# A hybrid decoder trunk on one Trainium2 core: the recurrent gate weights are fetched from ScalarE's queue, and the wide block products put their 512-column matmuls ahead of their 256-column ones

## The chip, the cores and the metric

The kernel runs on one core of one Trainium2 chip. The time is device microseconds (us) of one execution, and lower is better. Five engines work side by side, each in the order of its own list of instructions: TensorE (PE in the profile; its weight loads are the row PEld), VectorE (DVE), ScalarE (ACT), GpSimd (POOL) and SyncE (SP). They meet at semaphores: an instruction stands until the counts that it names are reached, and all that is behind it in its engine's list stands with it. Transfers (DMAs) are issued by an engine and carried by 16 shared DMA engines. SP and ACT issue into hardware queues (q1 and q10 in the profile), POOL into a software queue (q0); transfers that add into their target are all issued by POOL here.

## The reference, cut to what matters

One layer on 512 tokens of 1024 channels: a half-weighted SwiGLU feed-forward, a mixer of two branches, a second half-weighted SwiGLU, and a final norm, all in float32.

```python
for l in range(DEPTH):                                   # DEPTH = 1
    x = x + 0.5 * swiglu(rmsnorm(x, ffn1_norm[l]), ffn1_wg[l], ffn1_wu[l], ffn1_wd[l])
    x = x + hybrid_mixer(rmsnorm(x, mix_norm[l]), w_in[l], ...)
    x = x + 0.5 * swiglu(rmsnorm(x, ffn2_norm[l]), ffn2_wg[l], ffn2_wu[l], ffn2_wd[l])
return rmsnorm(x, final_norm)

def swiglu(x, w_gate, w_up, w_down):
    return (jax.nn.silu(x @ w_gate) * (x @ w_up)) @ w_down   # 1024 -> 2816 -> 1024

# in hybrid_mixer, the recurrent branch:
xr = causal_dwconv(xr, conv_w, conv_b)
r = jax.nn.sigmoid(block_diag_linear(xr, w_a, b_a))      # 16 blocks of 64 x 64
i = jax.nn.sigmoid(block_diag_linear(xr, w_x, b_x))
a = jnp.exp(-8.0 * r * softplus(-lam))
h = scan(h = a * h + jnp.sqrt(1 - a * a) * i * xr)
```

The mixer's other branch is an attention over the 128 keys of each query that an indexer picks; both branches are gated, added and projected.

## The kernel before, in words

**Precision.** Each float32 factor is split into a rounded high part and a rest. ACT makes the high part (names that end in h: `wh`, `xh`, `yh`, and `gw` for the gate weights' first half), DVE the rest (`wl`, `xl`, `yl`). Three matmuls then stand for one product: high by high, high by rest, rest by high. A matmul here has 128 rows of weights and 128, 256 or 512 moving columns.

**Stages.** The first feed-forward runs until about 355 us of the profiled execution, the mixer from there to about 700, the second feed-forward to the end. The last two carry most of this case.

**The mixer** is a list of 59 projection jobs (`ORDER`, L50; `run_jobs`, L1370). A job is 24 matmuls of 512 columns on one 512 KB block of weights, which SP fetches (`wr`), ACT rounds (`wh`) and DVE completes (`wl`); three raw buffers and three pairs of split buffers turn. Beside the jobs run small programs that hand work to the engines whenever a model of the engines' times (`Plan`, L85; `due`, L1180; `tick`, L1343) takes their inputs to be ready: the indexer's scores (`masks`, L1207, which multiplies the tiles `KI` and `QI`, takes the relu on ACT into `rl` and sums it on DVE into `am`), the attention heads (`head`, L1271: `pm`, `pth`), the recurrent branch (`recurrent`, L1528: `xc`, `xh`, `xl`) and the gate weights (`gate_weights`, L1150). The order is fixed when the program is built; the model only decides where in each list an instruction stands.

**The gate weights.** Eight times (t = 0 to 7), three jobs ahead of the job `x{t}`, `gate_weights` takes two slots, fetches 128 KB of weights into `gr`, lets ACT round them into the first half of `gw` and DVE put the rest into the second half. `recurrent` uses them in six matmuls of 512 columns (`mm<-xh,gw`). In the profile the fetch is POOL's line L158, `gr<-wrg`.

**POOL's queue.** During the mixer POOL also issues the transfers that build sums of the second feed-forward's weight blocks in HBM (`Blocks.stages`, L323: `scr<-w2u`, `scr<-scr`), each group waiting for the one before it.

**Hardware transfers and semaphores.** All transfers that SP and ACT issue share eight completion semaphores (DMAHW0 to DMAHW7), given out in the order in which the program was recorded. Before a transfer is issued, the earlier one on its semaphore must have landed, so a transfer stands until the one eight places ahead of it is in.

**The second feed-forward's first half** (`ffn_up`, L413, called with `blocks`) forms 18 pairs of weight blocks with seven products each, 126 products in all (`products`, L533). In such a wide product PE does, for j = 0 to 3, a matmul of 512 columns with `wh` (both halves of the moving tile `cm`) and one of 256 columns with `wl` (its first half), all into one PSUM bank. The first feed-forward calls the same function without `blocks` and uses 256 columns throughout.

Of the kernel before, what the change touches and what calls it, by code (L numbers as in the profile page):

```python
# [14 lines left out]
P = 128  # L15
S = 512
D = 1024
KD = D // P
# [157 lines left out]
def hybrid_kernel(ctx, tc, xt, vec, w1u, w1d, wm, wki, wrg, watt, wrnn, wout, w2u, w2d, gf, out):  # L176
    nc = tc.nc
    plan = Plan()
    V, A = plan.engine("DVE", nc.vector), plan.engine("ACT", nc.scalar)
    G, T = plan.engine("POOL", nc.gpsimd), plan.engine("PE", nc.tensor)  # L180
# [16 lines left out]
    moving = {}  # L197

    def nm(s):
        cnt[0] += 1  # L200
        return f"{s}_{cnt[0]}"

    def slot(dt=F32, name="s"):
        return plan.take("slot", big.tile([P, S], dt, tag="slot", name=nm(name)))
# [7 lines left out]
    def psum(tag="mm"):  # L212
        return psp.tile([P, S], F32, tag=tag, name=nm(tag))
# [71 lines left out]
    def waits(which, *tiles, aux=0, att=0, slots=0, key=None, mm=0, tmps=0, late=LATE):  # L285
        return which, tiles, aux, att, slots, key, mm, tmps, late
# [126 lines left out]
    def ffn_up(y, wu, n0, hs, g, waiting=(), given=(), ahead=None, blocks=None):  # L413
# [119 lines left out]
        def products(i):  # L533
            p, w = stream[i]
            o = ws[w]
            if p == 1:
                o.beta = psum("mm")
            elif p == 2:
                o.p2 = psum("aux")
            elif p == 5:  # L540
                o.gamma = psum("aux")
            both = {2: lambda: o.p2, 5: lambda: o.gamma, 3: lambda: o.gamma}.get(p, lambda: o.beta)()
            acc_ = both[:, lo]
            h, l = (t[:, i % 2 * H:(i % 2 + 1) * H] for t in units[i // 2])
            starts, opens = p in (1, 2, 5), dict(skip_group_check=p not in (1, 2, 5))
            for j in range(KD // 2):
                c = slice(j * P, (j + 1) * P)
                m = moving[{1: "n11", 2: "b21", 6: "t2", 5: "t1", 7: "r", 4: "q", 3: "n22"}[p]][j]
                if blocks:
                    T.matmul(both, h[:, c], m, start=starts and j == 0, stop=False, **opens)  # L550
                else:
                    T.matmul(acc_, h[:, c], m[:, lo], start=starts and j == 0, stop=False, **opens)
                    T.matmul(acc_, h[:, c], m[:, hi], start=False, stop=False, **opens)
                T.matmul(acc_, l[:, c], m[:, lo], start=False, stop=j == KD // 2 - 1, **opens)
# [98 lines left out]
        with tc.manual_schedule(engines=ENGINES):  # L653
# [34 lines left out]
            for i in range(len(stream)):  # L688
                products(i)
                if not i:  # L690
                    together(results_direct(len(direct) - 1))
                if blocks:
                    wide_step(i)
                elif i:
                    results(i - 1)
                if i + LEAD < len(stream):
                    if not blocks:
                        prepare(i + LEAD)
                elif not ahead or i + LEAD - len(stream) < PLAIN - f0:
                    halve(hs, f0 + i + LEAD - len(stream))  # L700
                if ahead:
                    ahead(i - len(stream))
                if i % 14 == 12 and i // 14 < f0:
                    halve(hs, i // 14)
                if blocks:
                    continue
                if i % 7 == 1 and len(ws) < count:
                    load_ = load(len(ws))
                next(load_, None)
# [214 lines left out]
    for k in range(KD):  # L924
        if k:
            Q.dma_start(x[k], xt[k])
        if k % CH == 0:
            c = slice(k * P, (k + CH) * P)
# [17 lines left out]
    for k in range(KD):  # L946
        y.append(norm_tile(k, V_G1, False))
        if k % CH == 0:
            c = slice(k * P, (k + CH) * P)
# [164 lines left out]
    with tc.manual_schedule(engines=ENGINES):  # L1114
# [3 lines left out]
        for i in range(last):  # L1118
            if i == 0:
                for k in ("pth", "ptl"):  # L1120
                    t = ptp.tile([P, NQ * S], F32, tag=k, name=nm("sm"))
# [28 lines left out]
    def gate_weights(t):  # L1150
        yield waits("PE", slots=2)
        r, w = slot(F32, "gr")[:, :2 * P], slot(F32R, "gw")
        h, l = w[:, :2 * P], w[:, 2 * P:]
        G.dma_start(r, wrg[t])
        yield waits("ACT", r)
        A.activation(h, r, AF.Copy)
        yield waits("DVE", h)
        V.tensor_sub(l, r, f(h))
        plan.drop(r)
        rgw[t] = h, l  # L1160
# [253 lines left out]
    for k in ("pth", "ptl"):  # L1414
        q = ptp.tile([P, NQ * S], F32R, tag=k, name=nm("QI"))
# [308 lines left out]
    for t in range(KD):  # L1724
        starts_.setdefault(max(0, order[f"x{t}"] - AHEAD), []).append(lambda t=t: gate_weights(t))
# [57 lines left out]
    def rows(m, half):  # L1783
        return xr[m // 2][:, m % 2, half * S:(half + 1) * S]
# [77 lines left out]
    with tc.manual_schedule(engines=ENGINES):  # L1862
# [19 lines left out]
        for m in range(2):  # L1882
            r = rows(m, 1)
# [66 lines left out]
```

## Time and profile before

| | us |
|---|---|
| three runs | 1075.64, 1078.17, 1075.22 |
| their median | 1075.64 |
| the profiled execution | 1079.05 |
| its span, from first to last instruction | 1077.2 |
| granted TensorE clock over the span | 0.995 |

The profiled execution is 3.4 us above the median of the runs, and 1.85 us of it lie outside its span. Busy time in the profile is a share of the span; an idle stretch is put down to whoever ended it. A row of the timeline has the start in us, the length in us, the engine, the line of the kernel, the operation, output<-inputs, and in brackets the idle time before it with its releaser. Where a helper records the operation, the line is that of the helper (L170 for computing, L158 for transfers), so tiles are told apart by name.

### The profile page before, as it was taken

What the parts mean: (1) busy time and instruction counts of PE and PEld (TensorE: products, weight loads), DVE (VectorE), ACT (ScalarE), POOL (GpSimd) and SP (SyncE); (2) the same over time, 40 slices, a digit from 0 to 9 for tenths busy, and PEclk for the clock granted to TensorE, in tenths of its full rate; (3) what the DMA queues carried; (4) which work ended last, traced back from release to release, by engine and by line L of the source; (5) the groups of instructions that cost most, each with busy time, mean ns of one, the idle gap of its engine ahead of it and who ended that gap; (6) DMA issues with size and microseconds to landing.
All of it is one profiled execution on the core that took longest, in us unless ns stands there. A gap on an engine that the chain in (4) does not pass through costs nothing.

```text
span 1077.2 us, 16865 instructions
## 1 busy us (share of the span) xinstructions
PE 1060.8 (98%) x5908; PEld 921.6 (86%) x5908; DVE 861.0 (80%) x1583; ACT 670.5 (62%) x1234; POOL 214.9 (20%) x283
## 2 busy tenths in 40 slices
PE   9999999999999999998999999999999999999997
PEld 7889999999999778886888888888888888888886
DVE  6687777779978878897889967765888888878865
ACT  6565555556566657865977574345666666666663
POOL 0161111102331113344443453000400000000020
PEclk9999999999999999999999999999999999999999
DMA  7297777738993597999999999433856565544673
GB/s 275 54 257 185 175 192 172 183 107 233 246 232 105 166 261 189 260 297 297 276 283 297 297 256 211 127 113 89 171 185 195 177 193 181 181 150 157 195 200 132
DMA packets 101012, 214.19 MB, mean 199 GB/s; under 512 B 12416, under 2 KB 20736, under 8 KB 100096
## 3 DMA queue, kind: packets, MB, share of 16 engines
q1 hardware_dynamic: 67632, 148.83, 42.2%
q0 software_dynamic: 32576, 63.46, 30.8%
q8 instruction: 46, 0.75, 0.3%
q10 hardware_dynamic: 720, 0.84, 0.2%
q14 instruction: 38, 0.31, 0.1%
HBM read 202.06 MB, written 56.62 MB: 240 GB/s over the span
## 4 chain that ended last, share of the span: by engine, by line
PE 78%; DMA 7%; DVE 6%; ACT 4%; issue 2%; POOL 1%; SPq 1%; ACTq 0%; POOLq 0%; DVEq 0%
PE mm L170 53%; PE aux L170 26%; DMA scr<-w2u 3%; DVE wl L170 2%; DMA gr<-wrg 1%; DMA sm<-w1d 1%; ACT wh L170 1%; DMA s<-w1d 1%; DMA QI<-qil 1%; SPq L158 1%; DVE ca L170 1%; DMA wr<-wm 0%; POOL scr L324 0%; DVE am L170 0%; DMA x<-xt 0%
## 5 line engine op out<-in xcount | busy, mean ns | idle before, releaser
L170 DVE TENSOR_TENSOR wl<-wr,wh 128x1024 fp32r<-128x1024 f32 (+2 forms) x253 | 258.0, 1023 | 88.5 <-ACT wh L170 86.4
L170 ACT ACTIVATE wh<-wr 128x1024 fp32r<-128x1024 f32 (+3 forms) x255 | 225.6, 890 | 82.0 <-PE aux L170 26.7
L170 PE MATMUL mm<-cm,wh 128*128 128x256 f32 (+1 forms) x1184 | 267.0, 311 | 0.6 <-ACT wh L170 0.3
L170 PE MATMUL mm<-cm,wl 128*128 128x256 f32 x736 | 207.8, 282 | 0.2 <-DVE wl L170 0.2
L170 PEld LDWEIGHTS mm<-cm,wh 128*128 128x128 f32 x1184 | 194.3, 191 | 15.4 <-ACT wh L170 0.5
L170 PE MATMUL mm<-yh,wh 128*128 128x512 f32 (+1 forms) x416 | 165.6, 398 | 2.0 <-ACT wh L170 1.4
L170 PE MATMUL mm<-yl,wh 128*128 128x512 f32 (+1 forms) x416 | 163.6, 394 | 0.5 <-DVE yl L170 0.5
L170 PE MATMUL mm<-yh,wl 128*128 128x512 f32 x408 | 160.6, 394 | 0.0
L170 PE MATMUL aux<-cm,wh 128*128 128x256 f32 (+1 forms) x664 | 160.2, 321 | 0.0
L170 PEld LDWEIGHTS mm<-cm,wl 128*128 128x128 f32 x736 | 140.4, 191 | 0.5 <-DVE wl L170 0.4
L170 PE MATMUL aux<-cm,wl 128*128 128x256 f32 x440 | 124.0, 282 | 0.0
L170 PEld LDWEIGHTS aux<-cm,wh 128*128 128x128 f32 x664 | 110.5, 191 | 10.1
L170 PEld LDWEIGHTS mm<-yh,wh 128*128 128x128 f32 (+1 forms) x416 | 78.8, 189 | 19.4 <-ACT wh L170 2.3
L170 PEld LDWEIGHTS mm<-yl,wh 128*128 128x128 f32 (+1 forms) x416 | 78.3, 188 | 16.3 <-DVE yl L170 1.2
L170 PEld LDWEIGHTS mm<-yh,wl 128*128 128x128 f32 x408 | 77.4, 190 | 16.8
L324 POOL DMA_DIRECT2D scr<-w2u x72 | 61.5, 965 | 113.6 <-DMA scr<-w2u 102.2
L170 PEld LDWEIGHTS aux<-cm,wl 128*128 128x128 f32 x440 | 83.8, 190 | 0.0
L158 POOL DMA_DIRECT2D cm<-h x16 | 13.8, 863 | 270.2 <-ACT cm L170 257.3
L170 PE MATMUL mm<-wh,cm 128*128 128x512 f32 x192 | 59.1, 389 | 0.0
L170 DVE TENSOR_TENSOR wl<-s,wh 128x512 fp32r<-128x512 f32 x72 | 49.3, 687 | 11.8 <-ACT wh L170 11.0
L170 ACT ACTIVATE wh<-s 128x512 fp32r<-128x512 f32 x72 | 43.7, 622 | 18.2 <-DVE s L170 14.5
L158 POOL DMA_DIRECT2D s<-w1u x32 | 30.1, 1105 | 108.8 <-DMA s<-w1u 51.3
(251 smaller groups left out, 2034.1 us busy)
## 6 DMA issues: line engine op xcount, KB each, us to landing
wr<-scr SPq DMA_DIRECT2D x104, 256.0 KB, 3.0
wr<-wm SPq DMA_DIRECT2D x39, 512.0 KB, 7.6
scr<-w2u POOLq DMA_DIRECT2D x72, 256.0 KB, 12.8
wr<-w2u SPq DMA_DIRECT2D x54, 256.0 KB, 3.0
scr<-scr POOLq DMA_DIRECT2D x52, 256.0 KB, 11.8
wr<-w1u SPq DMA_DIRECT2D x21, 512.0 KB, 5.1
wr<-w1d SPq DMA_DIRECT2D x18, 512.0 KB, 4.1
scr<-w2u SPq DMA_DIRECT2D x36, 256.0 KB, 9.1
```

The lines of the kernel that those rows point to most:

```text
L158: return self.engine.dma_start(out, src, **kw)
L170: return call(*args, **kw)
L324: plain, adds = nc.gpsimd.dma_start, lambda o, i: nc.gpsimd.dma_start(o, i, accum_op=ALU.add)
```

## The change

```diff
@@ -543,12 +543,12 @@
             acc_ = both[:, lo]
             h, l = (t[:, i % 2 * H:(i % 2 + 1) * H] for t in units[i // 2])
             starts, opens = p in (1, 2, 5), dict(skip_group_check=p not in (1, 2, 5))
-            for j in range(KD // 2):
+            ms = moving[{1: "n11", 2: "b21", 6: "t2", 5: "t1", 7: "r", 4: "q", 3: "n22"}[p]]
+            for j, m in enumerate(ms if blocks else ()):
+                T.matmul(both, h[:, j * P:(j + 1) * P], m, start=starts and j == 0, stop=False, **opens)
+            for j, m in enumerate(ms):
                 c = slice(j * P, (j + 1) * P)
-                m = moving[{1: "n11", 2: "b21", 6: "t2", 5: "t1", 7: "r", 4: "q", 3: "n22"}[p]][j]
-                if blocks:
-                    T.matmul(both, h[:, c], m, start=starts and j == 0, stop=False, **opens)
-                else:
+                if not blocks:
                     T.matmul(acc_, h[:, c], m[:, lo], start=starts and j == 0, stop=False, **opens)
                     T.matmul(acc_, h[:, c], m[:, hi], start=False, stop=False, **opens)
                 T.matmul(acc_, l[:, c], m[:, lo], start=False, stop=j == KD // 2 - 1, **opens)
@@ -1151,7 +1151,8 @@
         yield waits("PE", slots=2)
         r, w = slot(F32, "gr")[:, :2 * P], slot(F32R, "gw")
         h, l = w[:, :2 * P], w[:, 2 * P:]
-        G.dma_start(r, wrg[t])
+        nc.scalar.dma_start(r, wrg[t])
+        plan.copy(r, wrg[t], "POOL")
         yield waits("ACT", r)
         A.activation(h, r, AF.Copy)
         yield waits("DVE", h)
```

**The gate weights.** The eight transfers leave POOL's list and enter ACT's. The model of the engines' times still books them on POOL, so every other instruction keeps its place. On ACT's list, the place of the fifth transfer (t = 4, in the middle of the mixer) is this piece of the difference; `gw` is the rounding of the weights that `gr` brings, `wh` that of the next job's weights:

```order
 L170 ACTIVATE sg_5251<-mm_5174 128x512
 L170 ACTIVATE rl_5253<-aux_5212 128x512
+L1154 DMA gr_5265<-wrg 128x256
 L170 ACTIVATE gw_5266<-gr_5265 128x256
 L170 ACTIVATE wh_5276<-wr_5051 128x1024
```

The rounding that needs the transfer is now the instruction right behind its issue. The same on ACT at the seventh transfer (t = 6), which stands behind the gate `sg` of a finished job:

```order
 L170 ACTIVATE gu_5797<-gu_5797 128x512
 L170 ACTIVATE sg_5853<-mm_5809 128x512
+L1154 DMA gr_5862<-wrg 128x256
 L170 ACTIVATE gw_5863<-gr_5862 128x256
 L170 ACTIVATE wh_5872<-wr_5712 128x1024
```

Of the eight, t = 3 to 7 stand like this; at t = 0, 1 and 2 other work of ACT lies between. In the profile the moved transfer will carry its own line, L1154, as it no longer goes through the helper.

**The shared semaphores.** With eight more hardware transfers, the turn of DMAHW0 to DMAHW7 shifts for SP. Around the place where SP copies the indexer's queries into `QI`, one piece of SP's list before, with the semaphores that each transfer waits for:

```order
L158 DMA wr_4732<-wm 128x1024 [waits DMAHW5_49,DVE_49]
L158 DMA QI_4551<-qih_4645 32x512 [waits DMAHW6_49]
L158 DMA QI_4552<-qil_4683 32x512 [waits DMAHW7_49]
L158 DMA QI_4551<-qil_4646 32x512 [waits DMAHW0_49]
L158 DMA QI_4552<-qih_4682 32x512 [waits DMAHW1_49]
L158 DMA QI_4551<-qih_4645 32x512 [waits DMAHW2_49]
```

And the same transfers of SP in the changed kernel:

```order
L158 DMA wr_4732<-wm 128x1024 [waits DMAHW6_49,DVE_49]
L158 DMA QI_4551<-qih_4645 32x512 [waits DMAHW7_49]
L158 DMA QI_4552<-qil_4683 32x512 [waits DMAHW0_49]
L158 DMA QI_4551<-qil_4646 32x512 [waits DMAHW1_49]
L158 DMA QI_4552<-qih_4682 32x512 [waits DMAHW3_49]
L158 DMA QI_4551<-qih_4645 32x512 [waits DMAHW4_49]
```

SP skips DMAHW2, which one of ACT's transfers holds there: seven of SP's own transfers can be under way at such a place, where it was eight.

**The wide products.** On PE's list, the first product of the second feed-forward's stream (`cm` moving, `wh` and `wl` as weights):

```order
 L170 MATMUL mm_8647<-cm_8330,wh_8552 128x512
+L170 MATMUL mm_8647<-cm_8331,wh_8552 128x512
+L170 MATMUL mm_8647<-cm_8503,wh_8552 128x512
+L170 MATMUL mm_8647<-cm_8584,wh_8552 128x512
 L170 MATMUL mm_8647<-cm_8330,wl_8553 128x256
-L170 MATMUL mm_8647<-cm_8331,wh_8552 128x512
 L170 MATMUL mm_8647<-cm_8331,wl_8553 128x256
-L170 MATMUL mm_8647<-cm_8503,wh_8552 128x512
 L170 MATMUL mm_8647<-cm_8503,wl_8553 128x256
-L170 MATMUL mm_8647<-cm_8584,wh_8552 128x512
 L170 MATMUL mm_8647<-cm_8584,wl_8553 128x256
```

The eight matmuls are the same; the four of 512 columns come first. All 126 wide products change in this way, and nothing else on PE. DVE's list is unchanged.

## The prediction

> **What bounds the kernel now.** I read the page's busy table first, then PE's waits, then the tile `gr`, then ACT and PE in order of time around each gate-weight transfer.
>
> ```profile
> PE 1060.8 (98%) x5908; PEld 921.6 (86%) x5908; DVE 861.0 (80%) x1583; ACT 670.5 (62%) x1234; POOL 214.9 (20%) x283
> ```
>
> TensorE is busy for 98% of the span, so only two things can move the end: PE's idle time, and the pace of its matmuls. PE's longest wait, in the view of waits for PE alone (total, times, longest), and the rows of the view of the tile `gr`:
>
> ```profile
> PE aux L170 <- ACT pm L170: 4.0, 2, 3.4
> ```
>
> ```profile
> DMA gr<-wrg: 10.5, 3
> ...
> DMA to landing us min/median/max: 2.4/7.2/13.6
> ```
>
> Three of the eight roundings kept ACT waiting for their transfer, 10.5 us together (t = 5, 6, 7). The last of them is PE's longest wait. First ACT, then PE, then the stretches around it with the granted clock in the third column from the end:
>
> ```profile
> 501.44 0.60 ACT L170 ACTIVATE sg<-mm 128x512 f32<-128x512 f32 x1 [2.16 <-PE mm L170]
> 506.99 0.42 ACT L170 ACTIVATE gw<-gr 128x256 fp32r<-128x256 f32 x1 [4.95 <-DMA gr<-wrg]
> ```
>
> ```profile
> 508.70 0.33 PE L170 MATMUL aux<-ident,pm 128*128 128x128 f32 x1 [3.39 <-ACT pm L170]
> ```
>
> ```profile
> 505.00:509.00 4.00, 0.61 (x4) 0.30 (x3) 0.43 (x1) 2.01 (x6) 1.33 (x2) 1.00 1.08 306
> 509.00:513.00 4.00, 4.00 (x13) 3.16 (x12) 3.83 (x11) 3.95 (x7) 2.19 (x4) 0.60 1.10 245
> ```
>
> ACT was free at 502.04 and stood until the transfer was in; `pm`, behind `gw` on ACT, was what PE needed. PE lost 3.39 us, and then some (1 - 0.60) x 4.00 = 1.6 us more, as the granted clock fell to 0.60. So the most that the moved transfers can give back here is about 5 us.
>
> **The wide products.** PE in order of time, the first and last rows of 98 pairs of a 512-column and a 256-column matmul; of 25 steps from 512 to 512 columns in the mixer; of 18 steps from 256 to 256 at the end of the first feed-forward:
>
> ```profile
> 799.63 0.40 PE L170 MATMUL mm<-cm,wh 128*128 128x512 f32 x1
> ...
> 834.25 0.40 PE L170 MATMUL mm<-cm,wh 128*128 128x512 f32 x1
> ```
>
> ```profile
> 367.99 0.39 PE L170 MATMUL mm<-yl,wh 128*128 128x512 f32 x1
> ...
> 373.65 0.39 PE L170 MATMUL mm<-yh,wl 128*128 128x512 f32 x1
> ```
>
> ```profile
> 349.50 0.28 PE L170 MATMUL mm<-cm,wl 128*128 128x256 f32 x1
> ...
> 351.66 0.28 PE L170 MATMUL mm<-cm,wl 128*128 128x256 f32 x1
> ```
>
> A pair takes 34.62 / 98 = 0.3533 us; a step between equal widths takes 5.66 / 25 = 0.2264 and 2.16 / 18 = 0.1200, together 0.3464. Alternating costs 7 ns a pair. A product is 4 x 0.3533 = 1.413 us now; with the widths grouped it has three steps of each kind and one pair's worth of changes, 3 x 0.2264 + 3 x 0.1200 + 0.3533 = 1.393. Over 126 products that is 126 x 0.0207 = **2.6 us less**. The bounds are 0 (the 7 ns belong to these operands, not to the alternation) and 3.5 us (126 x 4 x 0.0069). I take 2.6.
>
> **How long a transfer takes on ACT's queue (L).** The trace has none of this kind in the mixer. From the view of transfers, with size and median us from issue to landing:
>
> ```profile
> gr<-wrg POOLq DMA_DIRECT2D x8, 128.0 KB, 7.2
> ...
> out<-o ACTq DMA_DIRECT2D x2, 256.0 KB, 2.4
> wr<-w1u ACTq DMA_DIRECT2D x2, 128.0 KB, 4.7
> ```
>
> ```profile
> 470.00:490.00 20.00, 19.43 (x91) 15.75 (x90) 18.60 (x47) 11.08 (x27) 9.22 (x13) 1.00 1.08 304
> ```
>
> The low end is 2.4, with the DMA engines nearly idle at the end of the program; the high end is 7.2, in POOL's queue. At t = 5 and 6 the engines are full (a share of 1.08). I take L = 4.7: same queue, same size, issued beside SP's loads. The Trainium skill, "DMA: Bandwidth & Descriptors", section "Anatomy of one DMA", fits 2.0 us plus the bytes over 436 GB/s, an estimate of 2.3 us here; the 2.4 of the first `gr` agrees, the median of 7.2 does not, and by that fit the time would be the first rival's.
>
> **What L does at each place.** At t = 3 to 7 the rounding stands right behind the issue, so ACT now stands for all of L, where POOL had issued early.
>
> At t = 2, ACT's wait behind one weight rounding is covered by the 2.55 us that it idles for PE anyway; t = 0 and 1 have some 9 us of other work:
>
> ```profile
> 392.85 1.20 ACT L170 ACTIVATE QS<-mm 64x512 fp32r<-64x512 f32 x2 [2.55 <-PE mm L170]
> ```
>
> At t = 3 nothing waited. ACT and PE:
>
> ```profile
> 399.99 0.43 ACT L170 ACTIVATE gw<-gr 128x256 fp32r<-128x256 f32 x1
> ...
> 401.63 1.06 ACT L170 ACTIVATE wh<-wr 128x1024 fp32r<-128x1024 f32 x1 [0.94 <-DMA wr<-wm]
> ...
> 403.12 0.64 ACT L170 ACTIVATE rl<-aux 128x256 f32<-128x256 f32 x2
> ```
>
> ```profile
> 406.13 0.51 PE L170 MATMUL aux<-KI,QI 128*128 128x384 f32 x2
> ```
>
> Of 4.7 us, 0.94 are idle time, and PE takes the bank that `rl` frees 2.37 us after `rl` (406.13 - 403.76). The rest is 1.4 us if all else stays, 0 if the weights' landing sets `wh` anyway; I take 0.7.
>
> At t = 4 nothing waited either, but DVE stood behind the `wh` that follows `gw` on ACT, and has almost no slack afterwards. DVE, then PE:
>
> ```profile
> 427.09 1.23 DVE L170 TENSOR_TENSOR wl<-wr,wh 128x1024 fp32r<-128x1024 f32 x1 [2.05 <-ACT wh L170]
> ...
> 432.87 1.23 DVE L170 TENSOR_TENSOR wl<-wr,wh 128x1024 fp32r<-128x1024 f32 x1 [0.30 <-ACT wh L170]
> ...
> 443.18 0.68 DVE L170 TENSOR_TENSOR xl<-xc,xh 128x512 fp32r<-128x512 f32 x1
> ```
>
> ```profile
> 445.38 0.39 PE L170 MATMUL mm<-xl,gw 128*128 128x512 f32 x1
> ```
>
> PE needs `xl` 1.52 us after it is made. 4.7 - 0.30 - 1.52 = **2.9 us**.
>
> At t = 5 and 6, ACT:
>
> ```profile
> 469.83 1.20 ACT L170 ACTIVATE QS<-mm 64x512 fp32r<-64x512 f32 x2 [0.33 <-PE mm L170]
> 474.31 0.42 ACT L170 ACTIVATE gw<-gr 128x256 fp32r<-128x256 f32 x1 [3.28 <-DMA gr<-wrg]
> ...
> 481.69 0.60 ACT L170 ACTIVATE sg<-mm 128x512 f32<-128x512 f32 x1 [1.37 <-PE mm L170]
> 484.59 0.42 ACT L170 ACTIVATE gw<-gr 128x256 fp32r<-128x256 f32 x1 [2.30 <-DMA gr<-wrg]
> ```
>
> ```profile
> 486.30 0.91 PE L170 MATMUL aux<-ident,pm 128*128 128x128 f32 x3 [0.56 <-ACT pm L170]
> ```
>
> At t = 5, `gw` starts at 471.03 + 4.7 = 475.7 instead of 474.31; the 1.4 us vanish in the 1.37 that ACT idles for PE before `sg`: 0. At t = 6 it starts at 482.29 + 4.7 = 487.0 instead of 484.59. PE already waits for `pm` behind it, so **2.4 us** arrive whole. At t = 7 it starts at 502.04 + 4.7 = 506.74 instead of 506.99: **0.25 us gained**, the stall and the dip of the clock stay.
>
> **SP's semaphores.** SP copies the indexer's queries back to back, 0.63 us apart, and PE uses them soon:
>
> ```profile
> 390.20 0.59 SPq L158 DMA_DIRECT2D QI<-qih  x1
> 390.90 0.52 SPq L158 DMA_DIRECT2D wr<-wm  x1
> 391.46 0.51 SPq L158 DMA_DIRECT2D QI<-qil  x1
> ```
>
> ```profile
> DMA to landing us min/median/max: 2.7/5.0/6.4
> ```
>
> ```profile
> 392.65 0.64 PE L170 MATMUL aux<-KI,QI 128*128 128x256 f32 x4
> ```
>
> Eight in flight cover 8 x 0.63 = 5.0 us, just the copies' median to landing; seven cover 4.4. If landing takes as long as before, two rounds lose 0.6 each, and up to 6.4 - 4.4 = 2.0 at the slowest; if it shortens with fewer in flight, nothing. Bounds 0 and 2.0; I take 0.9.
>
> **The sum.** 0.9 + 0.7 + 2.9 + 0 + 2.4 - 0.25 = 6.65 us more in the mixer, 2.6 less in the second feed-forward: **+4.05 us**. The profiled execution's 1079.05 becomes 1083.1; the median of the runs, 1075.64, becomes **1079.7**. POOL's list loses eight issues, which gives nothing: no row has PE waiting for POOL's sums.
>
> **The rivals.**
>
> *Faster: the transfer lands fast in a queue of its own.* It leaves the tail of POOL's queue, and at t = 7 the gain is L against 4.95. With L = 2.4: t = 4 costs 0.6, t = 6 0.1, t = 7 gives 2.55, and the stall, then 0.8 us, no longer brings the clock down: 1.6 more. Sum -3.45, with the products -6.05: 1069.6. It decides at about L = 3.2, where the total is -3. For it speaks that ACT's queue is empty; against it that all queues share engines that are full.
>
> *No change: L near 3.8.* 0.7 + 0.3 + 2.0 + 1.5 - 1.15 = 3.3, less 2.6: 1076.3. The two parts cancel.
>
> *The grouping changes nothing,* because the 7 ns belong to the operands: 1082.3. Against it: equal widths run at the same pace in three stages with other operands.
>
> *The dip of the clock goes,* since the stall at t = 7 is 3.14 us instead of 3.39: 1.6 less, 1078.1. The measured dip is the row of 0.60 above. The Trainium skill, "TensorE: Matmul & The Clock Gate", section "What's actually happening", halves the clock after an idle window of some 3.4 us; the trace agrees so far (3.39 us, 0.60), and by that rule a slightly shorter stall may escape, while the window's phase is free.
>
> **How the numbers follow.** Chances: the forecast 0.42 (L from 4.4 to 6); fast landing 0.14; cancelling 0.30; grouping without effect 0.08; the dip gone 0.06. About 0.3%, 3.2 us, is what a measurement of this kernel can tell from no change. Slower 0.42 + 0.08 = 0.50; same 0.30 + 0.06 = 0.36; faster 0.14. The ends of L alone would give 1069.6 and, at 7.2, over 1090; eight times in ten I expect L between 3.1 and 5.8, which is 1072.5 to 1085.0.
>
> **What would show it.** In the changed kernel: `gr` on ACT's queue with a median landing of 4 to 5.5 us; ACT waiting for `gr` five to six times, over 20 us in all; a PE wait of about 3 us at t = 6 and of about 3 at t = 7; PE held behind `xl` or `rl` near 430 to 450; 512-column steps of 0.2264 in the wide products, and a stretch of 126 products 2.6 us shorter. A median landing under 3.2, or PE's wait at t = 7 gone, would make the forecast wrong; so would wide products that still take 1.413.

## The result and the profile after

The changed kernel takes 1091.94 us in the median of four runs (1087.66 to 1095.08), the kernel before 1075.53. The ratio is 1.0144 with a 95% interval of 1.0106 to 1.0183: 1.4% slower, and above the forecast range of 1072.5 to 1085.0. The profiled executions differ by 12.7 us (1091.73 against 1079.05). The profiled execution of before lies 3.5 us above the median of its runs (all runs of before lie between 1071.95 and 1081.69), so the other 3.7 us of the medians' difference is not in these two traces.

The view of the tile `gr` in the changed kernel, and PE's waits (total, times, longest):

```profile
  DMA gr<-wrg: 24.4, 5
...
DMA to landing us min/median/max: 2.2/5.2/8.0
```

```profile
PE aux L170 <- ACT pm L170: 10.1, 2, 5.1
PE mm L170 <- ACT wh L170: 2.3, 3, 1.5
PE aux L170 <- ACT rl L170: 2.0, 1, 2.0
```

ACT waited 24.4 us instead of 10.5 us for the gate weights, five times instead of three, and PE 10.1 us instead of 4.0 us for the `pm` behind them; a wait of 2.0 us for `rl` is new. ACT in order of time, at t = 3, 4, 5, 6 and 7: the issue of each transfer (ACTq) and the rounding that needs it, with ACT's idle time in brackets; at t = 3 also the `rl` right behind the rounding:

```profile
400.87 0.33 ACTq L1154 DMA_DIRECT2D gr<-wrg  x1
...
406.65 0.42 ACT L170 ACTIVATE gw<-gr 128x256 fp32r<-128x256 f32 x1 [4.70 <-DMA gr<-wrg]
406.97 0.36 ACT L170 ACTIVATE rl<-aux 128x256 f32<-128x256 f32 x1
...
429.38 0.34 ACTq L1154 DMA_DIRECT2D gr<-wrg  x1
...
432.06 0.42 ACT L170 ACTIVATE gw<-gr 128x256 fp32r<-128x256 f32 x1 [1.08 <-DMA gr<-wrg]
...
475.02 0.34 ACTq L1154 DMA_DIRECT2D gr<-wrg  x1
...
483.03 0.42 ACT L170 ACTIVATE gw<-gr 128x256 fp32r<-128x256 f32 x1 [6.82 <-DMA gr<-wrg]
...
487.92 0.34 ACTq L1154 DMA_DIRECT2D gr<-wrg  x1
...
494.21 0.42 ACT L170 ACTIVATE gw<-gr 128x256 fp32r<-128x256 f32 x1 [5.19 <-DMA gr<-wrg]
...
512.60 0.33 ACTq L1154 DMA_DIRECT2D gr<-wrg  x1
...
519.83 0.42 ACT L170 ACTIVATE gw<-gr 128x256 fp32r<-128x256 f32 x1 [6.64 <-DMA gr<-wrg]
```

From issue to rounding it took 5.8, 2.7, 8.0, 6.3 and 7.2 us. PE in order of time shows what of this arrives. First t = 3, the last row ahead of the stall and the first behind it:

```profile
404.98 0.40 PE L170 MATMUL mm<-yh,wl 128*128 128x512 f32 x1
407.39 0.48 PE L170 MATMUL aux<-KI,QI 128*128 128x384 f32 x1 [2.02 <-ACT rl L170]
```

The wait ends with the `rl` that starts at 406.97, right behind the rounding. In the kernel before, the same two matmuls follow one another:

```profile
403.63 0.40 PE L170 MATMUL mm<-yh,wl 128*128 128x512 f32 x1
403.87 0.33 PE L170 MATMUL aux<-KI,QI 128*128 128x384 f32 x1
```

The distance between the two traces grows from 1.35 us to 3.52 us there. At t = 6 and t = 7, where the kernel before has its rows at 486.30 and 508.70:

```profile
495.92 1.06 PE L170 MATMUL aux<-ident,pm 128*128 128x128 f32 x3 [5.00 <-ACT pm L170]
...
521.54 0.48 PE L170 MATMUL aux<-ident,pm 128*128 128x128 f32 x1 [5.07 <-ACT pm L170]
```

The distance is 9.62 us and 12.84 us. Between these places it grows a second time, because the clock falls after each stall. The stretches behind the three stalls, the granted clock in the third column from the end:

```profile
407.30:411.00 3.70, 3.61 (x9) 2.95 (x10) 3.20 (x6) 2.58 (x6) 0.00 (x0) 0.55 0.14 18
...
494.00:498.00 4.00, 2.08 (x6) 1.63 (x7) 3.27 (x10) 3.05 (x8) 1.62 (x2) 0.50 1.08 288
...
521.00:525.00 4.00, 3.46 (x9) 2.79 (x10) 2.99 (x10) 3.95 (x10) 2.07 (x4) 0.50 1.09 236
```

Followed matmul by matmul, the distance is 1.4 us ahead of t = 3 (0.6 of it is there before the indexer's queries are used); the stall there adds 2.2 and the clock 1.7; t = 4 and 5 add nothing; t = 6 adds 4.4 and the clock 1.5; t = 7 adds 1.7, and the clock 0.9 beyond its dip in the kernel before. That makes 13.8 us; the second feed-forward gives back 1.2, and 12.6 us are left at PE's last matmul.

### The profile page after: what moved, and what is told of

It is laid out like the page before. It is cut to its first block, busy times and chain, and to the rows that moved or that the text cites. A ratio compares the mean times of both kernels' runs of the same rounds, so it can differ in the third digit from the quotient of the medians.

```text
span 1090.0 us, 16858 instructions
## 1 busy us (share of the span) xinstructions
PE 1064.0 (98%) x5908; PEld 925.2 (85%) x5908; DVE 861.4 (79%) x1583; ACT 669.7 (61%) x1234; POOL 209.8 (19%) x275
## 4 chain that ended last, share of the span: by engine, by line
PE 85%; DVE 6%; DMA 6%; ACT 2%; issue 2%; SPq 0%; POOL 0%; ACTq 0%; POOLq 0%; DVEq 0%
PE mm L170 59%; PE aux L170 26%; DMA gr<-wrg 2%; DVE wl L170 2%; DMA sm<-w1d 1%; ACT wh L170 1%; DMA s<-w1d 1%; DMA cm<-cb 1%; DVE yl L170 0%; DMA x<-xt 0%; DVE yf L170 0%; DVE ca L170 0%; DVE h L170 0%; ACT cm L170 0%; ACT yh L170 0%
## 5 line engine op out<-in xcount | busy, mean ns | idle before, releaser
L170 PE MATMUL mm<-cm,wh 128*128 128x256 f32 (+1 forms) x1184 | 242.0, 310 | 0.5 <-ACT wh L170 0.5
L170 PEld LDWEIGHTS mm<-cm,wh 128*128 128x128 f32 x1184 | 189.4, 191 | 8.3 <-ACT wh L170 0.7
L170 PE MATMUL mm<-cm,wl 128*128 128x256 f32 x736 | 172.7, 282 | 0.2 <-DVE wl L170 0.2
L170 PE MATMUL aux<-cm,wh 128*128 128x256 f32 (+1 forms) x664 | 141.4, 319 | 0.3 <-DMA cm<-cb 0.3
L170 PEld LDWEIGHTS mm<-cm,wl 128*128 128x128 f32 x736 | 130.2, 191 | 6.6 <-DVE wl L170 0.4
L170 PEld LDWEIGHTS aux<-cm,wh 128*128 128x128 f32 x664 | 106.9, 191 | 5.4 <-DMA cm<-cb 0.5
L170 PE MATMUL aux<-cm,wl 128*128 128x256 f32 x440 | 97.7, 282 | 0.0
L324 POOL DMA_DIRECT2D scr<-w2u x72 | 65.8, 1062 | 116.5 <-DMA scr<-w2u 113.3
L170 PEld LDWEIGHTS aux<-cm,wl 128*128 128x128 f32 x440 | 76.1, 190 | 4.6
L158 POOL DMA_DIRECT2D cm<-h x16 | 13.7, 857 | 269.1 <-ACT cm L170 256.1
L170 DVE TENSOR_TENSOR wl<-s,wh 128x512 fp32r<-128x512 f32 x72 | 49.3, 688 | 11.8 <-ACT wh L170 11.0
## 6 DMA issues: line engine op xcount, KB each, us to landing
scr<-w2u POOLq DMA_DIRECT2D x72, 256.0 KB, 11.8
```

The source lines that it names most:

```text
L158: return self.engine.dma_start(out, src, **kw)
L170: return call(*args, **kw)
L324: plain, adds = nc.gpsimd.dma_start, lambda o, i: nc.gpsimd.dma_start(o, i, accum_op=ALU.add)
```

## The experiments

Each ratio below compares with runs of the kernel before on the same chip; their medians lie between 1076.2 and 1076.7 us.

### The two parts apart

The move alone has the old product loop and this edit:

```diff
-        G.dma_start(r, wrg[t])
+        nc.scalar.dma_start(r, wrg[t])
+        plan.copy(r, wrg[t], "POOL")
```

> Only the gate weights' transfers on ACT's queue, products in the old order. Theory: the whole loss is the move, and the grouping gave back 1.2 us (what the two traces show from 126 products). So 1093 us (1091.94 + 1.2), with the same places of loss on PE: about 1.4 us at the indexer's queries, 2 to 4 us at t = 3, over 4 us at t = 6, about 2 us at t = 7, products of 1.413 us. Rival one, the grouping gave 2.6 us and the move lost less than it seems: 1094.5. Rival two, the grouping gave nothing or cost time: 1092 or under.

Measured: 1089.95 us, ratio 1.0138 (1.0119 to 1.0157), 3 us under the expected 1093 and on the side of rival two. The grouping alone has the diff's product loop and the transfers on POOL:

> Only the grouping, the gate weights back on POOL's queue. Theory: 126 products at 1.403 instead of 1.413 us, 1.2 us less, 1074.3 us. Rival one, the grouping is worth the forecast 2.6 us and something else in the changed kernel hid it: 1072.9. Rival two, no effect: 1075.5.

Measured: 1077.35 us, ratio 1.0010 (0.9989 to 1.0030). The 1.2 us less that were expected are a ratio of 0.9989, just at the end of this interval; the 2.6 us of rival one, 0.9976, lie outside. So the move makes the whole loss, 13.7 us, and the grouping gains nothing that can be measured, with the move or without it.

The profile of the grouping alone answers one more question. PE at the first use of the indexer's queries, in the changed kernel, in the grouping alone, and in a later profile of the kernel before (b3):

```profile
394.75 0.35 PE L170 MATMUL aux<-KI,QI 128*128 128x256 f32 x1 [0.97 <-PE aux L170]
```

```profile
394.19 0.35 PE L170 MATMUL aux<-KI,QI 128*128 128x256 f32 x1 [0.98 <-DMA wr<-wm]
```

```profile
393.44 0.35 PE L170 MATMUL aux<-KI,QI 128*128 128x256 f32 x1 [0.47 <-DMA wr<-wm]
```

The stall of about 1 us stands here also without a shift of SP's semaphores, and the second profile of the move alone (e1b, below), whose semaphores are shifted, has no wait at this place. It comes and goes with the execution.

### Issue and use apart

The changed kernel, with the rounding kept back:

```diff
         plan.copy(r, wrg[t], "POOL")
+        for _ in range(12):
+            yield waits("SP")
         yield waits("ACT", r)
```

> The changed kernel, but each rounding gw is kept back for 12 turns of three matmuls of PE (about 8 us) behind the issue of its transfer on ACT; the order on all engines shifts a little by it. Theory: the loss is ACT standing for a transfer that was issued just ahead of its use, so ACT's waits for gr fall from 24.4 us to under 4 us, PE's waits for pm from 10.1 us to under 3 us, and the time to 1070 to 1076 us (1075.5 less 1.2 for the grouping, less up to 5 for the stall and the dip of before at t = 7, plus 1.4 for SP's semaphores). Rival, the loss is in SP's shared semaphores or in the traffic of ACT's queue whatever its place: over 1085.

Measured: 1075.99 us, ratio 0.9995 (0.9977 to 1.0012). The view of `gr` has no wait of any engine, though the transfers are no faster:

```profile
DMA to landing us min/median/max: 2.1/5.2/8.5
```

ACT at t = 7, 16 us from issue to rounding, and no idle time in brackets:

```profile
499.46 0.34 ACTq L1154 DMA_DIRECT2D gr<-wrg  x1
...
515.55 0.40 ACT L170 ACTIVATE gw<-gr 128x256 fp32r<-128x256 f32 x1
```

All of the loss is gone with the same queue, the same eight shared semaphores and the same landing times. The gain of up to 5 us that was expected at t = 7 did not come: the time is that of before. The reason stands at the end of this section.

The same with the old product order:

> As e3_apart, with the old product order: transfers on ACT's queue, each rounding kept back for 12 turns of three matmuls. Theory: no wait of ACT for gr, as there; the time is that of e3_apart (1075.99) within the scatter of the two orders, from -1.8 (pattern of 1.387) to +1.2 (pattern of 1.413): 1074 to 1077.5.

Measured: 1074.56 us, ratio 0.9982 (0.9965 to 0.9999), no wait for `gr`. And the same delay with the transfers left on POOL:

> The kernel before, transfers on POOL's queue as ever, but each rounding kept back for the same 12 turns. Theory: what matters is the distance between issue and use and not the queue, so the 10.5 us that ACT waits for gr in the kernel before fall under 5 us, PE's stall of 3.4 to 5 us at t = 7 goes, and the time is that of e6_apart_old within 0.3%. Rival: POOL's queue is in its own way (landing up to 15 us behind the sums), over 5 us of waiting stay, and e6_apart_old is 2 us or more faster.

Measured: 1076.98 us, ratio 1.0001 (0.9981 to 1.0021), no wait for `gr` either, with landings of up to 13.8 us. The distance between issue and use decides. The kernel with ACT's queue (1074.56) is 2.4 us (0.2%) faster than the one with POOL's: within the 0.3% of the theory, but also over the 2 us that the rival named. The rival's other sign, over 5 us of waiting, is absent and the two intervals overlap, so a difference between the queues of this size is not shown.

PE's stall at t = 7 is gone in all three kernels, and still the time is that of before. Their traces show where it went. From PE's waits with the transfers on POOL:

```profile
PE mm L170 <- ACT ath L170: 1.2, 1, 1.2
PE mm L170 <- DVE atl L170: 0.9, 1, 0.9
PE aux L170 <- ACT pth L170: 0.7, 1, 0.7
```

These waits, with one of 0.2 us for `ptl` about 3.1 us in all, stand between 652 and 661 us, at the attention heads; the stall that went was 3.39 us in the profile of before. All three kernels with the rounding kept back have them, and no other profile has. Keeping the rounding back thus took away one stall and made PE wait for the heads later; why the heads come later was not followed.

### Why the transfers are slow

The changed kernel, with the transfers that build the weight sums started behind job `x7`, in twice the density:

```diff
-                    due_sums = len(sum_groups) * (i + 1) // SUMJOBS
+                    due_sums = len(sum_groups) * max(0, i - 28) // (SUMJOBS - 29)
```

> The changed kernel, but POOL's and SP's transfers that build the weight sums (scr) start only behind job x7, in twice the density, so that none is under way while the eight gr are fetched; the order on PE, ACT and DVE is the same. Theory: gr took 5.7 to 8.0 us at t = 3, 5, 6 and 7 because the DMA engines were full of these sums; without them it lands in 2.4 to 4 us, ACT's waits for gr fall from 24.4 to under 13 us, and PE reaches the end of t = 7 at least 8 us earlier than in the changed kernel. Rival, the time belongs to ACT's queue itself: landing still 5 to 8 us. The time as a whole is not the point, since the sums may come too late for the second feed-forward; if they do not, 1080 to 1084.

Measured: 1129.31 us, ratio 1.0502 (1.0478 to 1.0526). The views of transfers from 395 to 525 us, in the changed kernel:

```profile
wr<-wm SPq DMA_DIRECT2D x19, 512.0 KB, 7.2
...
gr<-wrg ACTq DMA_DIRECT2D x5, 128.0 KB, 6.3
```

and without the sums:

```profile
wr<-wm SPq DMA_DIRECT2D x20, 512.0 KB, 3.6
gr<-wrg ACTq DMA_DIRECT2D x5, 128.0 KB, 2.4
```

The same five transfers on ACT's queue take 2.4 instead of 6.3 us, and SP's too take half the time. The busy share of the DMA engines is the last number but one in these rows, of the changed kernel and of the one without the sums:

```profile
470.00:490.00 20.00, 20.00 (x93) 16.70 (x93) 16.69 (x34) 11.48 (x22) 8.64 (x13) 1.00 1.07 289
```

```profile
470.00:490.00 20.00, 18.25 (x82) 14.78 (x81) 17.42 (x46) 9.47 (x24) 0.00 (x0) 0.96 0.33 106
```

ACT's waits for `gr` fall from 24.4 to 9.9 us, and PE's row at t = 7 stands at 508.23 instead of 521.54:

```profile
508.23 0.33 PE L170 MATMUL aux<-ident,pm 128*128 128x128 f32 x1 [1.01 <-ACT pm L170]
```

The traffic of the sums is the cause of the long landings. That it acts through the DMA engines, which all queues share, fits their busy share, 1.07 with the sums and 0.33 without; a limit of the memory behind them was not tested apart. The Trainium skill, "DMA: Bandwidth & Descriptors", section "Issuing engines are not separate DMA queues", says that transfers started by the scalar, sync or gpsimd engine run on the same 16 DMA engines and interleave; the landing times above, long with the sums' traffic and short without it whichever engine issued, agree. Delaying the sums is no cure: they then come too late, and PE waits 17.8 us in all for `cm<-cb` and 17.3 us for `wh` further on.

Last, the transfers in SP's list instead of ACT's:

```diff
-        G.dma_start(r, wrg[t])
+        nc.sync.dma_start(r, wrg[t])
+        plan.copy(r, wrg[t], "POOL")
```

> Old product order; the gate weights' transfers stand in SP's list instead of ACT's, at the places in which they are recorded; everything else as in the move alone. Theory (the DMA engines are full, and the rounding stands just behind the issue): landing about as long, 5 to 8 us at t = 3, 5, 6, 7, ACT's waits for gr over 15 us, time 1083 to 1095. Rival (it is ACT's own queue that is slow, or ACT's being late to issue): waits for gr under 10.5 us, 1072 to 1077.

Measured: 1103.79 us, ratio 1.0250 (1.0205 to 1.0295), worse than expected by either. Landing took 6.5 us in the median, up to 10.0, but ACT waited 44.0 us for it, eight times. The second cause is SP's list around t = 6:

```profile
480.09 1.14 SPq L1397 DMA_DIRECT2D scr<-w2u  x2
491.27 4.53 SPq L158 DMA_DIRECT2D wr<-wm  x2
495.86 0.60 SPq L1154 DMA_DIRECT2D gr<-wrg  x1
```

SP issued nothing from 481.2 to 491.3 us, and `gr` stood behind the transfers that waited. This goes back to ACT's wait at t = 5: the rounding there started only at 488.62, the weights' rounding behind it at 488.94, DVE completed them at 491.25, and with that the raw buffer was free that the transfer at 491.27 needs.

### Which places cost

The move alone, but t = 6 and 7 on POOL (e7), and the opposite, only t = 6 and 7 on ACT (e10; the condition is turned round):

```diff
-        G.dma_start(r, wrg[t])
+        if t > 5:
+            G.dma_start(r, wrg[t])
+        else:
+            nc.scalar.dma_start(r, wrg[t])
+            plan.copy(r, wrg[t], "POOL")
```

> Old product order; t = 0 to 5 on ACT's queue, t = 6 and 7 on POOL's as before. Theory: the loss at t = 6 and t = 7 is that of their own two transfers, 4.3 + 1.7 us and 3.1 + 0.9 us in the profile of the move alone, so about 10 of its 13.7 us come back: 1078 to 1081 us. Rival: ACT's lateness at t = 3 to 5 is carried on into t = 6 and 7, and under half comes back: 1084 or more.

> Old product order; only t = 6 and 7 on ACT's queue, t = 0 to 5 on POOL's as before. Theory: these two alone cost 8 to 11 us against the kernel before: 1084 to 1087. Rival: without the lateness of t = 3 to 5 they cost under 5 us: under 1081.

Measured: 1078.69 us, ratio 1.0023 (1.0004 to 1.0043), and 1088.14 us, ratio 1.0109 (1.0065 to 1.0152). PE's waits for `pm`, in e7 and in e10:

```profile
PE aux L170 <- ACT pm L170: 2.7, 2, 1.8
```

```profile
PE aux L170 <- ACT pm L170: 11.6, 2, 6.3
```

The last two transfers cost 11.8 us by themselves, 1.1 more than the upper end of what was expected; the first six cost 2.3. Together that is 14.1 us, about the 13.7 of the move alone, so little is carried over from place to place.

### The pace of the wide products

The grouping had been priced from one profile. The move alone, with the old order, shows another pace. The first and the last row of a stretch of PE in the profile of before, then in that of the move alone:

```profile
819.77 0.40 PE L170 MATMUL mm<-cm,wh 128*128 128x512 f32 x1
...
930.01 0.40 PE L170 MATMUL aux<-cm,wh 128*128 128x512 f32 x1
```

```profile
819.69 0.39 PE L170 MATMUL mm<-cm,wh 128*128 128x512 f32 x1
...
929.93 0.39 PE L170 MATMUL aux<-cm,wh 128*128 128x512 f32 x1
```

In the same 110.24 us there are 312 pairs and 318 pairs: 0.3533 and 0.3467 us a pair, 1.413 and 1.387 us a product. The latter is the sum of the steps between equal widths, 0.2264 + 0.1200 = 0.3464; in that execution alternating costs nothing. The grouped order, in the changed kernel, 78 products from first to last row:

```profile
821.74 1.09 PE L170 MATMUL mm<-cm,wh 128*128 128x512 f32 x4
...
931.20 1.09 PE L170 MATMUL mm<-cm,wh 128*128 128x512 f32 x4
```

109.46 / 78 = 1.403 us. Five profiles were taken to see where the pace comes from: the kernel before twice more, the move alone again, and the kernel before with another number of warming matmuls.

> The kernel before once more, for a second profile. Question: is the pace of the wide products a property of the order (512, 256 in turn) or of the execution? The two profiles of the old order so far show 1.413 us a product (before) and 1.387 (the move alone); four profiles of the grouped order all show 1.4035. Theory: the order falls into one of several repeating patterns in each execution, so this one may show 1.387 as well as 1.413, and then the time of the old order scatters by 126 x 0.026 = 3.3 us from this alone. Rival: the kernel fixes it; 1.413 again.

> The kernel before a third time, for its profile. The old product order has shown two repeating patterns: 1.413 us a product in both profiles of this kernel, 1.387 in the four other programs that keep the order (the move alone, SP's list, and the two with rounding kept back). Theory: the pattern belongs to the program (where its instructions stand on PE, for their order in this stage is the same), so 1.413 again. Rival: it is drawn in each execution by the timing at the start of the stage; then 1.387 is as likely.

> The move alone once more. By the theory that the pattern belongs to the program: 1.387 us a product again, and a stage of 175.5 us from its first to its last wide matmul. By the rival: 1.413 and 178.5 us is as likely. Landings of gr at t = 3, 5, 6, 7 again 5 to 8 us, ACT's waits for them over 20 us.

```diff
-WARM = 8
+WARM = 7
```

> The kernel before with 7 instead of 8 warming matmuls at the very start (their result is never used), so that every later instruction of PE stands one matmul earlier in its list; nothing else differs. If the pattern belongs to the place of the instructions, it may change to 1.387 us a product, and the time is then up to 3 us below the kernel before (1073); if it is set by the order or by the waits alone, 1.413 stays and the time is that of before.

> The same with 9 warming matmuls. Place: 1.387 or 1.413 by the place, and the same in every execution of one program; with w7 and the kernel before it gives three neighbouring places. Order and waits alone: 1.413.

Measured: both profiles of before show 1.413 (1074.65 and 1079.15 us), and so does the second of the move alone (1087.65 us), which had shown 1.387:

```profile
819.67 0.40 PE L170 MATMUL aux<-cm,wh 128*128 128x512 f32 x1
...
929.91 0.40 PE L170 MATMUL aux<-cm,wh 128*128 128x512 f32 x1
```

These are 312 pairs in 110.24 us. (Its transfers did as expected, with 24.9 us of ACT's waits, but for a landing of 4.1 us at t = 3.) So one program shows both, and the theory that the program fixes the pace falls. The kernels with 7 and 9 warming matmuls show 1.387; 7 gives 1075.58 us, ratio 1.0000 (0.9981 to 1.0019), 9 gave 1073.78 us in one run. Over all twelve profiles of the old order, six show 1.413 (before three times, the move alone once, e7, e10) and six 1.387 (the move alone once, e5, e6, e8, 7 and 9 warming matmuls). The grouped order showed 1.403 in each of its four profiles. Over 126 products that is 176.4 us for the mean of the old order and 176.8 for the new: nothing to gain on average, a gain of 1.3 us in one half of the executions and a loss of 2.1 in the other. What chooses between the two patterns was not found.

## Why the prediction was wrong, point by point

**Two steps failed: the transfer's time L, and the clock behind the stalls, which was left out.** Between the forecast of +4.05 us and the 12.6 us of the traces lie 8.55 us: 4.1 from dips of the clock that had no term, 2.55 net from the places that hang on L (1.5 at t = 3, 2.0 at t = 6 and 1.95 at t = 7 more, 2.9 at t = 4 less), 1.4 from the grouping, and 0.5 from what lies ahead of t = 3 (1.4 measured against the 0.9 for SP's semaphores).

**The transfer's time, L = 4.7 us.** It came from two transfers of the same size and queue at the program's start, which took 3.6 and 5.8 us. The prediction had 7.2 as the other end, and at t = 5 and 6 it had the DMA engines full. Its low end of 2.4 comes from the program's end, where their busy share is 0.33 over the last 17 us, so no row that it used was taken under full engines on a hardware queue. The measured L at t = 5, 6 and 7 was 8.0, 6.3 and 7.2. Queue and size did not decide, but what else was under way did (the kernel with late sums), and the trace of before had rows of that kind. Its view of transfers from 470 to 520 us, another hardware queue, same stretch:

```profile
wr<-wm SPq DMA_DIRECT2D x8, 512.0 KB, 8.2
...
scr<-w2u SPq DMA_DIRECT2D x9, 256.0 KB, 10.4
```

The nearest row was the one that shares the stretch, not the one that shares the queue, though these transfers are larger and would have priced L somewhat high. With L = 7.2 the prediction's own terms give 4.9 us instead of 2.4 at t = 6 (measured 4.4) and 2.25 instead of -0.25 at t = 7 (measured 1.7). That its total for 7.2, over 1090, is close to the 1091.94 measured is in part luck: that total has 5.4 us at t = 4, which did not come, and none of the 4.1 us of dips, which did.

**The mechanism was right.** The rounding stands behind its issue, ACT stands for all of L, and PE follows through `pm` at t = 6 and 7: the kernels with issue and use apart lose nothing, and the two places alone cost 11.8 us.

**The term left out: the clock after the new stalls.** The dip was priced at t = 7, for the stall that was there already, and not for the stalls that the change would make or lengthen. These dips cost 1.7 us at t = 3, 1.5 at t = 6 and 0.9 more at t = 7, 4.1 of the 12.6 us.

**t = 3** was put at 0.7 and came to 2.2, through `rl` behind `gw` as named, but not through the pair of rows that was priced. The prediction took its slack of 2.37 us from the `rl` behind the weights' rounding; PE waited for the one ahead of that rounding (406.97), where ACT's 0.94 us of idle time cannot help. In the trace of the move alone the same place costs 0.7 us, without a dip.

**t = 4** was put at 2.9 and came to 0 in the changed kernel, where L was 2.7; the prediction's own terms still give 0.9 for that. Where L was 4.3 to 4.6 there (both profiles of the move alone, and e7), PE does wait for `xl`, as named; the row of the move alone:

```profile
PE mm L170 <- DVE xl L170: 0.8, 1, 0.8
```

The path was right, and its size about a third of the 2.5 to 2.7 us that the terms give for these L.

**t = 5** was put at 0, and is 0 even with L = 8.0. The 1.37 us of idle time that were named cannot cover that L, so there was more slack than the prediction had read.

**SP's semaphores**, 0.9: PE's wait of 0.97 at the named place is there, but the grouping alone has it without any shift of semaphores, a profile of before has half of it, and one of the move alone has the shift without the wait. The term is not supported; it was not tried by itself.

**The grouping**, 2.6 us less, was 1.2 in these two traces and about nothing on average. The 7 ns belong neither to the alternation nor, as the rival had it, to the operands: the same order on the same operands runs with them in one execution and without them in the next.

**The rivals.** Fast landing and the cancelling case needed an L that, of t = 3 to 7, only t = 4 had. "The dip goes" rested on a slightly shorter stall; the stall at t = 7 became longer.

## What to carry to other kernels

Price a moved transfer by those that land in the same stretch, whichever queue they use, and count distance between issue and use before the choice of queue: twelve turns of distance took away all waits for these transfers on either queue. When a change makes PE stall, give the slow clock that may follow a term of its own: here it was 4.1 of 12.6 us. When a cure removes a stall and the time stays, look for the wait that took its place. A pace of some nanoseconds a step needs more than one profiled execution before it is made a term.

## What the runs showed of the hardware

**The length of a stall alone does not tell whether the clock dips.** The stall of 2.02 us at t = 3 of the changed kernel was followed by a granted clock of 0.55 (shown above). In the kernel with late sums a stall of 1.75 us at 486.7 us was followed by 0.50 from 488.3 to 491.7 us. In the second profile of the kernel before, a stall of 3.07 us was followed by full speed; its row, and the stretch behind it:

```profile
505.68 0.33 PE L170 MATMUL aux<-ident,pm 128*128 128x128 f32 x1 [3.07 <-ACT pm L170]
```

```profile
507.00:511.00 4.00, 4.00 (x20) 3.30 (x19) 3.90 (x10) 3.94 (x8) 2.91 (x5) 1.00 1.11 215
```

The Trainium skill, "TensorE: Matmul & The Clock Gate", section "What's actually happening", has the clock halve after at least one idle window of some 3.4 us whose phase is free. A stall that escapes agrees with that; a dip after 2.02 or 1.75 us does not, as no such window fits into it, and the measurement decides.

**A stream of matmuls keeps one of several paces.** Alternating matmuls of 512 and 256 columns ran through nearly the whole stage at 0.3533 or at 0.3467 us a pair, and which one changed between executions of the same program.
